# A hybrid attention layer on one core: one ring of six then five load buffers, query and key scalings one step later, distance tables off GpSimd

## The chip, the cores and the metric

The kernel runs on one core of a Trainium2 chip. The metric is the device time of one execution in microseconds (us). The engines are called as the profile calls them: PE is the matmul engine (TensorE), DVE the vector engine (VectorE), ACT the scalar engine (ScalarE), POOL is GpSimd, and SP is the engine (SyncE) whose queue issues the loads.

## The reference

One decoder layer on 256 tokens of width 2048, in float32. A modulation from `c` shifts, scales and gates a normalized input; one projection of 9296 columns feeds two attention groups of eight heads and an indexer of 16 small heads; both groups are gated, joined and projected out.

```python
mod = jax.nn.silu(c) @ w_ada + b_ada
shift, scale, gate = jnp.split(mod, 3, axis=-1)
h = _rms_norm(x, g_norm) * (1.0 + scale[:, None, :]) + shift[:, None, :]
proj = h @ w_in
qa, ka, va, za, q_idx, k_idx, w_idx, qb, kb, vb, zb = jnp.split(proj, COL_SPLITS, axis=-1)
qa = _rms_norm(qa.reshape(heads_a), q_norm_a)      # likewise ka, qb, kb; k_idx over its 64 columns
ya = _dsa_attention(qa, ka, va, q_idx, k_idx, w_idx, _alibi_slopes(N_HEADS_A))
yb = _moba_attention(qb, kb, vb, _alibi_slopes(N_HEADS_B))
ya = ya.reshape(B, L, D_A) * jax.nn.silu(za)
yb = yb.reshape(B, L, D_B) * jax.nn.silu(zb)
y = jnp.concatenate([ya, yb], axis=-1) @ w_out
return x + gate[:, None, :] * y
```

Inside both attentions a score is `q k / sqrt(128) - slope * distance`, masked to the past, with slopes 1/2, 1/4, ... 1/256. The A group sees only the 64 keys that the indexer scores highest for each query. With 256 tokens the B group has one block, so it is plain causal attention.

## The kernel before

**Loads and weights.** All weights come in loads of at most 1 MB, numbered in a fixed order and issued from SP's queue into `raw` buffers (line 244 on, function `issue`). Most loads are pieces of `w_in` or `w_out`, four row tiles of 512 columns each. Others are rows of the transposed `w_ada`; for these one DVE instruction (L289, in the profile CUSTOM_DVE_ANT_0, here called the row product) multiplies a row with silu(c) and adds it up. A weight load is cut into slices of two row tiles, numbered `wh0`, `wl0`, `wh1` and so on: ACT casts a slice to `wh` (L322), DVE subtracts to get the rest `wl` (L332), and PE does three matmuls for each pair of row tile and token tile (L774 to L776), twelve in a slice. ACT and DVE work two slices ahead of PE (`LA = 2`).

**Buffers for loads.** There are four `raw` buffers in one pool and two in a second pool, `rawe`, that only some of the early rows of `w_ada` use. When the indexer starts, `rawe` is closed and its room goes to the small tiles of indexer and heads.

**Work between the slices.** Everything else is written as generators that are stepped between two slices: `idx_k` and eight `idx_pair`s (the indexer; `qi` is a copied query pair, `lg` its matmuls, `rl` their relu), `prep` (norms of queries and keys), `prep_z` and `head`. `yield n` makes a generator skip n further slices. A scheduler then places the written instructions on each engine, so an instruction can stand a little before or behind its place in the text. In `prep` the squares go to ACT (L506), the power -1/2 to GpSimd (L149 and L150), and the eight scalings to ACT (L513):

```python
rsqrt(ssq[:, 8:16], ssq[:, 0:8], HD)
yield 1
...
nc.scalar.activation(s, s, AF.Copy, scale=ssq[:, 8 + 4 * t + h:9 + 4 * t + h])
```

**A head.** `head` transposes queries and keys on PE (`tr`), multiplies them (`s`, L540 and L541), subtracts the slope times the distance on DVE (`ns`, L545) with a table `nb` that GpSimd has made for this head (L536), takes the exponential on ACT (L548), transposes (`pt`, L554), multiplies with the values (`pv`, L563) and makes `yT`, which the output projection needs. Heads are named by group, half and number: `b00` is the first, `a13` the last.

## Time and profile before

| | us |
|---|---|
| Time, median of three runs | 575.06 |
| The three runs | 574.56, 575.06, 578.45 |
| The profiled execution's own time | 578.7 |
| Its span, first to last instruction | 576.9 |
| PE busy | 553.6 |
| DVE busy | 444.5 |
| ACT busy | 319.6 |
| POOL busy | 48.0 |

The span is 1.8 us shorter than the own time of the same execution; nothing in the trace covers that rest. The profiled execution is 3.6 us above the median of the three timed runs and near the longest of them. Busy times of different engines overlap, so they don't add up to the span.

### The profile page before, as it was taken

The numbers are of one execution on the slowest core, as the hardware profiler recorded it, in microseconds if no ns is written. First come the engines' busy times: TensorE is split into PE (matmuls) and PEld (weight loads), VectorE is DVE, ScalarE is ACT, GpSimd is POOL, SyncE is SP. The second block draws the span as 40 slices with busy tenths as digits, with TensorE's granted clock in tenths as the row PEclk, the third lists the DMA queues.
The fourth block names the chain that finished last, engine by engine and source line by source line (L and its number), as shares of the span: only waits on it lengthen the run. The fifth ranks groups of instructions, "written<-read, shape, count | busy, mean of one in ns | idle before, by whom it ended". The sixth has DMA issues, their size and how long they took to land.

```text
span 576.9 us, 7456 instructions
## 1 busy us (share of the span) xinstructions
PE 553.6 (96%) x2658; PEld 462.7 (80%) x2658; DVE 444.5 (77%) x683; ACT 319.6 (55%) x652; POOL 48.0 (8%) x62
## 2 busy tenths in 40 slices
PE   3889999999999999999799999999999999999996
PEld 2769888888889988976577888888888888887885
DVE  4877789898898898998689996678787576458452
ACT  4588563544444353576555566646776785554340
POOL 4100000000000000102201002111110210000000
PEclk9999999999999999999989999999999999999999
DMA  8999998898898987877845376767675468445611
GB/s 293 412 350 370 361 346 326 330 360 285 314 359 318 366 326 270 268 298 279 303 152 177 129 275 235 273 221 265 226 255 201 148 231 279 146 150 190 244 37 38
DMA packets 59670, 150.09 MB, mean 260 GB/s; under 512 B 3056, under 2 KB 9456, under 8 KB 53616
## 3 DMA queue, kind: packets, MB, share of 16 engines
q1 hardware_dynamic: 58480, 147.51, 71.1%
q10 hardware_dynamic: 1152, 2.10, 1.2%
q8 instruction: 21, 0.34, 0.2%
q14 instruction: 17, 0.14, 0.1%
HBM read 147.50 MB, written 2.10 MB: 259 GB/s over the span
## 4 chain that ended last, share of the span: by engine, by line
PE 87%; ACT 4%; DVE 2%; POOL 2%; issue 2%; DMA 1%; SPq 0%; DVEq 0%; ACTq 0%
PE mm_y_o L774 5%; PE mm_y_o L776 5%; PE mm_y_o L775 5%; PE mm_h_zb L776 3%; PE mm_h_zb L774 3%; PE mm_h_zb L775 3%; PE mm_h_za L775 3%; PE mm_h_i L776 3%; PE mm_h_i L775 3%; PE mm_h_i L774 3%; PE mm_h_qb L774 3%; PE mm_h_za L776 3%; PE mm_h_qb L776 3%; PE mm_h_qb L775 3%; PE mm_h_qa L774 3%; PE mm_h_ka L775 2%
## 5 line engine op out<-in xcount | busy, mean ns | idle before, releaser
L322 ACT ACTIVATE wh<-raw 128x1024 fp32r<-128x1024 f32 (+3 forms) x192 | 188.2, 990 | 140.5 <-PE mm_y_o L776 32.9
L332 DVE TENSOR_TENSOR wl<-raw,wh 128x1024 fp32r<-128x1024 f32 (+3 forms) x192 | 215.0, 1140 | 60.5 <-ACT wh L322 59.9
L289 DVE CUSTOM_DVE_ANT_0 raw<-raw,s_row 128x2048 f32<-128x2048 f32 (+1 forms) x49 | 110.2, 2250 | 14.1 <-DMA raw<-in_w_ada_t 14.1
L774 PE MATMUL mm_y_o<-wh,yT 128*128 128x512 f32 x128 | 51.7, 404 | 0.0
L775 PE MATMUL mm_y_o<-wl,yT 128*128 128x512 f32 x128 | 49.9, 390 | 0.0
L776 PE MATMUL mm_y_o<-wh,yT 128*128 128x512 f32 x128 | 49.8, 390 | 0.0
L774 PE MATMUL mm_h_i<-wh,hhi 128*128 128x384 f32 (+1 forms) x96 | 31.7, 330 | 0.0
L775 PE MATMUL mm_h_i<-wl,hhi 128*128 128x384 f32 (+1 forms) x96 | 31.5, 328 | 0.0
L536 POOL TENSOR_SCALAR nbb<-dist 128x384 f32<-128x384 f32 x8 | 8.0, 1001 | 283.3 <-DVE mmod L289 211.2
L776 PE MATMUL mm_h_i<-wh,hlo 128*128 128x384 f32 (+1 forms) x96 | 31.4, 329 | 0.0
L776 PEld LDWEIGHTS mm_y_o<-wh,yT 128*128 128x128 f32 x128 | 24.0, 188 | 5.4 <-DVE yT L575 0.2
L774 PEld LDWEIGHTS mm_y_o<-wh,yT 128*128 128x128 f32 x128 | 24.1, 188 | 4.7 <-ACT yT L574 0.2
L775 PEld LDWEIGHTS mm_y_o<-wl,yT 128*128 128x128 f32 x128 | 24.1, 188 | 4.6
L774 PE MATMUL mm_h_qa<-wh,hhi 128*128 128x512 f32 x64 | 25.6, 409 | 0.9 <-ACT wh L322 0.9
L774 PE MATMUL mm_h_zb<-wh,hhi 128*128 128x512 f32 x64 | 26.4, 412 | 0.0
L774 PE MATMUL mm_h_vb<-wh,hhi 128*128 128x512 f32 x64 | 26.4, 412 | 0.0
L775 PE MATMUL mm_h_za<-wl,hhi 128*128 128x512 f32 x64 | 25.1, 392 | 0.9 <-DVE wl L332 0.9
L774 PE MATMUL mm_h_kb<-wh,hhi 128*128 128x512 f32 x64 | 25.7, 405 | 0.0
L775 PE MATMUL mm_h_zb<-wl,hhi 128*128 128x512 f32 x64 | 25.7, 401 | 0.0
L775 PE MATMUL mm_h_vb<-wl,hhi 128*128 128x512 f32 x64 | 25.6, 400 | 0.0
L774 PE MATMUL mm_h_qb<-wh,hhi 128*128 128x512 f32 x64 | 25.5, 401 | 0.0
L774 PE MATMUL mm_h_za<-wh,hhi 128*128 128x512 f32 x64 | 25.5, 406 | 0.0
(216 smaller groups left out, 1227.3 us busy)
## 6 DMA issues: line engine op xcount, KB each, us to landing
raw<-in_w_in SPq DMA_DIRECT2D x51, 1024.0 KB, 5.9
raw<-in_w_ada_t SPq DMA_DIRECT2D x47, 1024.0 KB, 6.2
raw<-in_w_out SPq DMA_DIRECT2D x16, 1024.0 KB, 5.0
raw<-in_w_in SPq DMA_DIRECT2D x17, 512.0 KB, 3.6
raw<-in_w_in SPq DMA_DIRECT2D x11, 768.0 KB, 4.6
x<-in_x SPq DMA_DIRECT2D x8, 256.0 KB, 6.9
xr<-in_x ACTq DMA_DIRECT2D x8, 256.0 KB, 6.5
raw<-in_w_in SPq DMA_DIRECT2D x3, 672.0 KB, 7.4
```

The costliest lines, as they stand in the source:

```text
L289: nc.vector.tensor_tensor_reduce(out=ld["v"], in0=ld["v"], in1=s_row[:, h0:h1], scale=1.0, scalar=0.0, op0=ALU.mult, op1=ALU.add, accum_ou ...
L322: nc.scalar.activation(hi[:, :n, :w], v, AF.Copy)
L332: nc.vector.tensor_tensor(lo[:, :n, :w], v, sb["hi"][:, :n, :w].bitcast(F32), op=ALU.subtract)
L536: nc.gpsimd.tensor_scalar(nb, dista if q[0] == "a" else dist, 2.0 ** -(hid + 1), 0.0, op0=ALU.mult, op1=ALU.add)
L774: nc.tensor.matmul(ps, a_hi, sb["hi"][:, i, :w], start=st, stop=False)
L775: nc.tensor.matmul(ps, a_hi, sb["lo"][:, i, :w], start=False, stop=False)
L776: nc.tensor.matmul(ps, a_lo, sb["hi"][:, i, :w], start=False, stop=en)
```

## The change

Five things change together.

1. The load buffers are one ring. Up to the indexer load n takes one of six buffers in turn (four of the first pool, two of the second, by `n_issued % 6`). From there on it is one of five: the four, and one that is taken from the room of the small tiles.
2. That room comes from tiles that now share one pair of buffers, tag `qk`: the indexer's `qi`, the tanh tiles `th`, the heads' `qk` and the output's products `o`. The squares of x at the start write to the large pool of `u` tiles instead.
3. `prep` yields 2 instead of 1 before its scalings.
4. The heads' distance tables `nb` are gone. DVE reads the plain distances and multiplies the sum by a constant per head (`scale=`).
5. To make up for that constant, the factor on the keys (`gneg`) is now a table of eight columns, one per head, made by GpSimd at the start: eight memsets and two products, where DVE had two.

```diff
```diff
@@ -45,5 +45,2 @@
 
-EARLY = {1, 2} | set(range(5, 2 * KT + KT * KT))
-
-
 NO_WAIT = mybir.DependencyInfo(mybir.DependencyClass.NoSync, mybir.DependencyReason.DATA)
@@ -139,7 +136,11 @@
         nc.gpsimd.tensor_scalar(one, one, 1.0, None, op0=ALU.add)
+
     gneg = {}
+    steep = consts.tile([P, 8], F32, name="steep")
+    for h in range(8):
+        nc.gpsimd.memset(steep[:, h:h + 1], -(HD ** -0.5) * 2.0 ** (h + 1))
     for i, g in enumerate("ab"):
-        gt = consts.tile([P, 1], F32, name=f"gneg{g}")
-        nc.vector.scalar_tensor_tensor(gt, cc[:, 64 + 2 * i:65 + 2 * i], -(HD ** -0.5),
-                                       cc[:, 65 + 2 * i:66 + 2 * i], op0=ALU.mult, op1=ALU.mult)
+        gt = consts.tile([P, 8], F32, name=f"gneg{g}")
+        nc.gpsimd.tensor_scalar(gt, steep, cc[:, 64 + 2 * i:65 + 2 * i], cc[:, 65 + 2 * i:66 + 2 * i],
+                                op0=ALU.mult, op1=ALU.mult)
         gneg[g] = gt
@@ -246,5 +247,7 @@
             ld = loads[n_issued]
-
-            pool = rawe if ld["kind"] == "ada" and ld["to"][0] == "mod" and n_issued - n_start in EARLY else rawp
-            raw = pool.tile([P, 2048], F32, tag="raw", name=f"raw{n_issued}")
+            pool = rawe if not late_pool and n_issued % 6 > 3 else rawp
+            if late_pool and n_issued % 5 == 4:
+                raw = late_pool[0].tile([P, 2048], F32, tag="raw", bufs=1, name=f"raw{n_issued}")
+            else:
+                raw = pool.tile([P, 2048], F32, tag="raw", name=f"raw{n_issued}")
             if ld["kind"] == "ada":
@@ -352,3 +355,3 @@
         for j in range(4):
-            junk = work.tile([P, 512], F32, name=f"junkx{t}{j}", tag="big", bufs=2)
+            junk = u_tile(f"junkx{t}{j}")
             with in_order():
@@ -466,3 +469,3 @@
             nc.tensor.transpose(pt[:, t * P:(t + 1) * P], proj[g, t][:, c:c + P], ident)
-        qi = late_tiles().tile([P, L], F32, name=f"qi{p}", tag="qi")
+        qi = late_tiles().tile([P, 512], F32, name=f"qi{p}", tag="qk", bufs=2)[:, :L]
         nc.scalar.activation(qi, pt[:, :L], AF.Copy)
@@ -508,3 +511,3 @@
         rsqrt(ssq[:, 8:16], ssq[:, 0:8], HD)
-        yield 1
+        yield 2
         for t in range(2):
@@ -518,3 +521,3 @@
             z = proj["z" + q, t]
-            th = work.tile([P, 512], F32, name=f"th{q}{t}", tag="big", bufs=2)
+            th = late_tiles().tile([P, 512], F32, name=f"th{q}{t}", tag="qk", bufs=2)
             nc.scalar.activation(th, z, AF.Tanh, scale=0.5)
@@ -533,6 +536,5 @@
         nc.vector.tensor_copy(qk[:, :L], pt[:, :L])
-        nc.scalar.activation(qk[:, L:], pt[:, L:], AF.Copy, scale=gneg[q[0]])
-        nb = late_tiles().tile([P, 384], F32, name="nb" + name, tag="nb", bufs=2)
-        nc.gpsimd.tensor_scalar(nb, dista if q[0] == "a" else dist, 2.0 ** -(hid + 1), 0.0,
-                                op0=ALU.mult, op1=ALU.add)
+
+        nc.scalar.activation(qk[:, L:], pt[:, L:], AF.Copy, scale=gneg[q[0]][:, hid:hid + 1])
+        far = dista if q[0] == "a" else dist
         yield 1
@@ -544,3 +546,4 @@
         for t, lo, hi in ((0, 0, P), (1, P, 384)):
-            nc.vector.tensor_tensor_reduce(out=ns[:, lo:hi], in0=ps[:, lo:hi], in1=nb[:, lo:hi], scale=1.0,
+            nc.vector.tensor_tensor_reduce(out=ns[:, lo:hi], in0=ps[:, lo:hi], in1=far[:, lo:hi],
+                                           scale=2.0 ** -(hid + 1),
                                            scalar=3e38, op0=ALU.add, op1=ALU.min, accum_out=st[:, t:t + 1])
@@ -684,3 +687,3 @@
                 for c in range(0, 512, w):
-                    tmp = work.tile([P, 512], F32, name=f"o{n}{t}{c}", tag="big", bufs=2)
+                    tmp = late_tiles().tile([P, 512], F32, name=f"o{n}{t}{c}", tag="qk", bufs=2)
                     nc.vector.tensor_tensor(tmp[:, :w], ps[:, c:c + w], gate_bc[n][:, c:c + w], op=ALU.mult)
```
```

**Where instructions stand now.** Up to about 236 us of the trace the rows of ACT, DVE and SP are the same, apart from the start. Behind that many rows move by one slice. Line numbers below are each kernel's own, three higher in the changed one.

On ACT, around the key norms of the first B half (`jkb` squares, `p_kb` scalings, `qi3` the fourth of the later indexer pairs, for whose matmuls `lg6` PE waits), before:

```order
L506 ACTIVATE jkb013_2532,sskb0_2517<-p_kb0_1_775 128x128
L513 ACTIVATE p_kb0_0_773<-p_kb0_0_773,sskb0_2517 128x128 x3
L468 ACTIVATE qi3_2559<-ptq3_2556 128x256
L513 ACTIVATE p_kb0_0_773<-p_kb0_0_773,sskb0_2517 128x128
L513 ACTIVATE p_kb0_1_775<-p_kb0_1_775,sskb0_2517 128x128 x4
L322 ACTIVATE wh106_2605<-raw98_2398 128x1024
L322 ACTIVATE wh107_2626<-raw98_2398 128x1024
L477 ACTIVATE rl6_2580<-lg6_2577 128x384
L477 ACTIVATE rl7_2587<-lg7_2584 128x384
L322 ACTIVATE wh108_2668<-raw99_2451 128x1024
```

And in the changed kernel:

```order
L509 ACTIVATE jkb013_2541,sskb0_2526<-p_kb0_1_784 128x128
L516 ACTIVATE p_kb0_0_782<-p_kb0_0_782,sskb0_2526 128x128 x2
L325 ACTIVATE wh106_2606<-raw98_2399 128x1024
L471 ACTIVATE qi3_2568<-ptq3_2565 128x256
L516 ACTIVATE p_kb0_0_782<-p_kb0_0_782,sskb0_2526 128x128 x2
L516 ACTIVATE p_kb0_1_784<-p_kb0_1_784,sskb0_2526 128x128 x4
L325 ACTIVATE wh107_2635<-raw98_2399 128x1024
L480 ACTIVATE rl6_2589<-lg6_2586 128x384
L480 ACTIVATE rl7_2596<-lg7_2593 128x384
L325 ACTIVATE wh108_2667<-raw99_2460 128x1024
```

The copy `qi3` still stands behind the first scalings; in front of it there are now two scalings and the cast `wh106`, where there were three scalings.

On PE, the last head, `a13` (some matmuls `mm_y8` of the slices 172 and 174 between these rows are left out), before:

```order
L540 MATMUL sa13_4733<-qka13_4685 128x128
L541 MATMUL sa13_4733<-qka13_4685 128x256
L563 MATMUL pva12_4760<-pTa12_4712,p_va1_0_557 128x256
L565 MATMUL pva12_4760<-pTa12_4712,p_va1_1_559 128x128
L568 MATMUL pva12_4760<-ident_81,p_za1_1_472 128x128
L554 MATMUL pta13_4775<-ident_81,nsa13_4736 128x128 x3
L774 MATMUL mm_y8_o1_0_4566<-wh174_4744,yT4_4588 128x512
L776 MATMUL mm_y8_o1_1_4567<-wh174_4744,yT4_4588 128x512
L774 MATMUL mm_y8_o1_0_4566<-wh174_4744,yT5_4677 128x512
L563 MATMUL pva13_4784<-pTa13_4779,p_va1_0_557 128x256
L568 MATMUL pva13_4784<-ident_81,p_za1_0_470 128x128
```

And in the changed kernel:

```order
L557 MATMUL pta12_4701<-ident_81,nsa12_4642 128x128 x3
L542 MATMUL sa13_4728<-qka13_4682 128x128
L543 MATMUL sa13_4728<-qka13_4682 128x256
L566 MATMUL pva12_4741<-pTa12_4705,p_va1_0_566 128x256
L568 MATMUL pva12_4741<-pTa12_4705,p_va1_1_568 128x128
L557 MATMUL pta13_4752<-ident_81,nsa13_4731 128x128
L778 MATMUL mm_y8_o1_0_4538<-wl174_4714,yT4_4585 128x512
L557 MATMUL pta13_4752<-ident_81,nsa13_4731 128x128 x2
L779 MATMUL mm_y8_o1_0_4538<-wh174_4712,yT4_4585 128x512
L778 MATMUL mm_y8_o1_1_4539<-wl174_4714,yT4_4585 128x512
L566 MATMUL pva13_4761<-pTa13_4756,p_va1_0_566 128x256
L568 MATMUL pva13_4761<-pTa13_4756,p_va1_1_568 128x128
```

All twelve matmuls of slice 172 stood between `sa13` and `pta13`, and now stand ahead of `sa13`; three matmuls of slice 174 stand between the last of `pta13` and `pva13`, where there were seven.

On SP, loads 101 to 108, before:

```order
L276 DMA raw101_2536<-in_w_in 128x4x512
L276 DMA raw102_2599<-in_w_in 128x4x512
L253 DMA raw103_2601<-in_w_ada_t 128x2048
L276 DMA raw104_2666<-in_w_in 128x4x512
L276 DMA raw105_2730<-in_w_in 128x4x512
L253 DMA raw106_2732<-in_w_ada_t 128x2048
L276 DMA raw107_2797<-in_w_in 128x2x512
L276 DMA raw108_2869<-in_w_in 128x4x512
```

And in the changed kernel:

```order
L279 DMA raw101_2545<-in_w_in 128x4x512
L279 DMA raw102_2600<-in_w_in 128x4x512
L256 DMA raw103_2602<-in_w_ada_t 128x2048
L279 DMA raw105_2728<-in_w_in 128x4x512
L256 DMA raw106_2730<-in_w_ada_t 128x2048
L279 DMA raw104_2665<-in_w_in 128x4x512
L279 DMA raw107_2793<-in_w_in 128x2x512
L279 DMA raw108_2853<-in_w_in 128x4x512
```

Load 104, the first to use the buffer from the small tiles' room, is now issued behind 105 and 106.

## Rows read from the trace of the kernel before

**Rows 1.** The page: shares by engine, granted clock in 40 slices, the chain by engine.

```profile
PE 553.6 (96%) x2658; PEld 462.7 (80%) x2658; DVE 444.5 (77%) x683; ACT 319.6 (55%) x652; POOL 48.0 (8%) x62
...
PE 87%; ACT 4%; DVE 2%; POOL 2%; issue 2%; DMA 1%; SPq 0%; DVEq 0%; ACTq 0%
```

**Rows 2.** Waits of the matmul queue, by cause: total us, times, longest us.

```profile
PE lg L474 <- ACT qi L468: 4.4, 2, 3.2
...
PE sb L540 <- ACT rl L477: 0.3, 1, 0.3
PE ptk L457 <- ACT kk L452: 0.2, 1, 0.2
```

**Rows 3.** Busy us of each engine by window, granted clock, DMA share, GB/s.

```profile
0.00:20.00 20.00, 8.37 (x34) 7.59 (x35) 10.91 (x24) 9.86 (x24) 7.99 (x28) 1.00 0.89 326
...
260.00:280.00 20.00, 18.87 (x98) 13.98 (x97) 17.44 (x25) 13.35 (x34) 2.59 (x2) 1.00 0.86 312
280.00:300.00 20.00, 16.61 (x78) 12.37 (x77) 12.49 (x21) 10.32 (x26) 4.18 (x2) 0.91 0.55 180
340.00:560.00 220.00, 219.94 (x1054) 183.14 (x1053) 150.14 (x252) 133.13 (x320) 24.76 (x22) 1.00 0.61 212
560.00:577.00 17.00, 12.51 (x56) 10.02 (x54) 5.20 (x8) 1.07 (x2) 0.00 (x0) 0.93 0.09 32
```

**Rows 4.** Timeline of PE around the longest wait: start us, us, instruction.

```profile
282.91 0.39 PE L776 MATMUL mm_h_vb<-wh,hlo 128*128 128x512 f32 x1
286.54 0.50 PE L474 MATMUL lg<-kiT,qi 64*128 64x128 f32 x4 [3.24 <-ACT qi L468]
```

**Rows 5.** Timeline of ACT, key squares to the fourth copy of the indexer.

```profile
280.46 0.30 ACT L506 ACTIVATE jkb<-p_kb 128x128 f32<-128x128 f32 x1
...
285.24 0.98 ACT L513 ACTIVATE p_kb<-p_kb,sskb 128x128 f32<-128x128 f32 x3 [4.39 <-POOL sskb L150]
286.13 0.36 ACT L468 ACTIVATE qi<-ptq 128x256 f32<-128x256 f32 x1
```

**Rows 6.** Timeline of GpSimd (POOL): powers of eight columns.

```profile
260.17 2.51 POOL L150 TENSOR_TENSOR ssqb<-ssqb,mhalf 128x8 f32<-128x8 f32 x1
...
281.26 3.94 POOL L150 TENSOR_TENSOR sskb<-sskb,mhalf 128x8 f32<-128x8 f32 x1
...
361.62 1.64 POOL L150 TENSOR_TENSOR sskb<-sskb,mhalf 128x8 f32<-128x8 f32 x1
```

**Rows 7.** Timeline of DVE beside the second of these powers.

```profile
281.43 2.28 DVE L289 CUSTOM_DVE_ANT_0 raw<-raw,s_row 128x2048 f32<-128x2048 f32 x1
```

**Rows 8.** Two windows around the longest wait, with the granted clock.

```profile
288.00:292.00 4.00, 4.00 (x14) 3.10 (x12) 3.07 (x5) 2.59 (x4) 0.00 (x0) 0.57 0.02 6
```

**Rows 9.** Timeline of ACT: query scalings, and what follows them.

```profile
262.71 2.45 ACT L513 ACTIVATE p_qb<-p_qb,ssqb 128x128 f32<-128x128 f32 x8 [3.02 <-POOL ssqb L150]
265.07 1.05 ACT L322 ACTIVATE wh<-raw 128x1024 fp32r<-128x1024 f32 x1
...
268.65 0.37 ACT L468 ACTIVATE qi<-ptq 128x256 f32<-128x256 f32 x1
```

**Rows 10.** Groups of GpSimd: the distance tables of the A heads.

```profile
L536 POOL TENSOR_SCALAR nba<-dista 128x384 f32<-128x384 f32 x8 | 8.5, 1066 | 60.6 <-DVE sta L545 44.1 <-DVE stb L545 16.5
```

**Rows 11.** Timeline of GpSimd at the start.

```profile
2.72 1.78 POOL L139 TENSOR_SCALAR cc<-cc 128x1 f32<-128x1 f32 x9 [0.59 <-DMA cc<-in_cols]
...
11.24 0.19 POOL L149 TENSOR_SCALAR rx<-rx 128x1 f32<-128x1 f32 x1 [5.54 <-DVE rx L358]
```

**Rows 12.** Timeline of PE, last head: scores, transposes, products.

```profile
514.79 0.38 PE L540 MATMUL sa<-qka 128*128 128x128 f32 x2
...
521.23 0.67 PE L563 MATMUL pva<-pTa,p_va 128*128 128x256 f32 x2
```

**Rows 13.** Timeline of ACT, last head: second exponential.

```profile
516.49 0.49 ACT L548 ACTIVATE nsa<-nsa,sta 128x256 f32<-128x256 f32 x1
```

**Rows 14.** DMA issues: weight loads, KB each, median us to landing.

```profile
raw<-in_w_in SPq DMA_DIRECT2D x51, 1024.0 KB, 5.9
```

## The prediction

> **What bounds the kernel now.** I read the page's shares first. PE is busy 553.6 of 576.9 us, and 87% of the chain that ended last is PE [rows 1]. So a change pays only where it takes idle time of PE away or gives PE less work, and this one gives PE the same matmuls. The windows say where the idle time lies [rows 3]: 11.63 us in the first 20 us and 4.49 us in the last 17. Neither stretch loses or gains a step on its path, as worked out below. Of the 23.3 us in all this leaves 7.2 us. From 340 to 560 us PE is idle for 0.06 of 220 us, so no weight, load or head is late there. The piece that matters is 260 to 300 us: 1.13 us idle in its first half and 3.39 us in its second.
>
> The waits name the cause [rows 2]: the indexer's matmuls `lg` wait twice for ACT's copy `qi`, 4.4 us together. The longer wait is 3.24 us: `lg6` starts at 286.54 [rows 4]. Followed back: `qi3` is at 286.13 behind three key scalings, and those start at 285.24 after ACT has stood 4.39 us for GpSimd's power; the last squares began at 280.46 [rows 5]. The power was issued at 281.26 and took 3.94 us, while the same power later takes 1.64 us (five times of eight) [rows 6]. Beside it DVE runs a row product from 281.43, for 2.28 us [rows 7]; 1.64 and 2.28 make 3.92, so the power seems to have run behind the row product. After this idle time the clock is granted at 0.57 for four microseconds [rows 8], the lower of its two levels for most of them, which costs 4 x 0.43 = 1.7 us. The stall's whole price is 3.24 + 1.7 = 4.9 us. The window with the shorter wait keeps 1.00 [rows 3].
>
> **Which time the sum starts from.** These rows are of an execution of 578.7 us, 3.6 us above the median and 0.2 us from the longest timed run. The part of the stall that comes from the slow power is 3.94 - 1.64 = 2.3 us, with the clock 4.0 us. That is near 3.6, and the row product started only 0.17 us behind the power. My estimate is that in the two shorter runs the power came first. This is argued, not shown. I make the sum against 578.7 and carry the difference over to 575.06.
>
> **The change part by part.**
>
> Six buffers in one ring, five later. A buffer that is free earlier lets a load start earlier, and that pays only where PE waits for weights. At 0 to 20 us the DMA share is 0.89 [rows 3] and behind that PE waits for nothing that a load brings, save under 2 us; from 340 us on PE has no idle time to give back. I take 0, bounds -0.5 and 0; what covers it is the slices cast two ahead. The cost that it could have is a rival below.
>
> Shared small tiles. `qi`, `th`, `qk` and `o` take turns in two buffers. Each is read within a slice of being written and the next use comes a slice or more later by the order. 0, bounds 0 and 0.4, the length of one `qi` [rows 5].
>
> The factor table. GpSimd gets eight memsets and two products of eight columns. The nearest rows are nine one-column operations in 1.78 us and one of 0.19 us, before which GpSimd stood 5.54 us [rows 11]. Ten times 0.2 is 2 us and fits into the 5.54, so 0; without that cover 2 us would stand in front of the first transposes. DVE loses two tiny operations there: 0.
>
> No distance tables. GpSimd loses 16 operations, 8.5 us for the eight of the A heads [rows 10] and about as much for the others. They were off PE's path, and DVE's operation keeps its shape with another constant. 0 on the path, bounds -0.3 and 0.
>
> Scalings later. Here the order decides, not the number in the yield.
> Query side: `wh100` stood behind the eight query scalings and now stands in front of them, where ACT stood 3.02 us for the power. The cast takes 1.05 us [rows 9]. So `qi1`, at 268.65 after an unbroken row of ACT work, comes up to 1 us earlier, and the wait of 4.4 - 3.24 = 1.16 us falls to some 0.5. But what PE wins here it loses at the next wait unless that one moves too.
> Key side: everything ahead of the squares may run up to 1 us earlier, for the same cast; I take 0.8, since DVE and ACT were without a pause there only in part. Against that `qi3` has the same place behind the power, and in front of it stand two scalings and `wh106` in place of three scalings: 1.05 - 0.98/3 = 0.7 us later. Seen from the start, `lg6` moves by -0.8 + 0.7 = -0.1 us. With the wait for `kk` (0.2 us [rows 2]), whose transposes go one slice later, I take -0.3, bounds -1.3 and +0.7. The power still has the row product behind it, so 3.24 + 1.7 stay in the execution profiled.
>
> A page of the Trainium skill speaks of this pair: "SBUF — State Buffer", section "Who interferes with whom", says that a DVE instruction with two inputs from SBUF and a GpSimd instruction that reads SBUF share a port pair as an exclusive lock, which the first to start holds to its end. By it the power, 0.17 us ahead, should have taken 1.64 us and the row product waited; here the row product took its 2.28 and the power 3.94. By the rule the stall would be 3.24 - 2.3 = 0.9 us, the clock's loss would be gone with it, and this execution would have been near 574.7. The row decides; the issue time of a power may not be the time at which it reads.
>
> Heads one slice later. `sb00` no longer stands in the middle of a crowded slice: its wait of 0.3 us [rows 2] goes, -0.3. At the end it gets tight. Before, scores of `a13` started at 514.79, the second exponential ended at 516.49 + 0.49 = 516.98, and `pva13` came at 521.23 [rows 12, 13]; twelve matmuls filled the time between scores and exponential. Now only `pva12` and one matmul lie there, some 1.1 us against the 2.2 that the chain takes for the last two of the three transposes. I take +0.4 for it, bounds 0 and 2.2.
>
> The sum: -0.3 - 0.3 + 0.4 = -0.2 us. From 578.7 this gives 578.5, and from the median **574.9 us**. The bounds added are -2.4 and +3.0.
>
> **The rivals.**
>
> *The collision goes away (A).* If the new order lets the power run ahead of the row product in all executions, the profiled one gains 4.0 + 0.2 us and comes to 574.5; the median gains only as far as it had the collision, so 570.9 at the best (575.06 - 4.2). For it: 0.17 us is a small distance. Against it: the squares and the row product both hang on the same cast, so they keep their distance. By the Trainium skill's rule on the shared ports ("SBUF — State Buffer", "Who interferes with whom") this is what would happen wherever the power starts first.
>
> *The scalings leave `qi3`'s way (B).* If `qi3` did not wait for the power, all of 4.9 us, 1.16 us and 0.5 us of small waits would go: 575.06 - 6.6 = 568.5. Against it: the order of ACT shows two scalings still in front of `qi3`.
>
> *The collision becomes the rule (C).* Then the median is what the profile is now, 578.5.
>
> *Slower: load 104 is late (D).* It is issued behind 105 and 106, the first of which needs a buffer that a weight slice frees and the second one that a row product frees, and a load takes 5.9 us to land [rows 14]. Between 280 and 300 us DMA is busy 0.55 and DVE 12.49 of 20 us [rows 3], so there is room. It decides once load 104 comes later than the slices ahead of PE last; two loads of 5.9 us are 11.8, of which some 6 would stand on PE, with the clock's 1.7 us: 575.06 + 7.7 = 582.8.
>
> *The change doesn't do what it says (E).* Neither ring nor yield reaches PE and only the tables go; 575.1. In size this can't be told from the forecast.
>
> **How the numbers follow.** Forecast with E 0.64 (572.5 to 577.5), A 0.12, B 0.06, C 0.10, D 0.08. The likeliest time is 574.9. The range leaves out B and D, 0.14, and takes in A and C: 570.5 to 578.6. One per cent is 5.75 us, about what a measurement of this kernel can tell from no change. Faster by more, under 569.3, is B and little else: 0.08. Slower by more, over 580.8, is D with a bad case of C and the tight end: 0.09. Within: 0.83.
>
> **What would show it.** In the changed kernel's profile `lg` should still wait for `qi` for 2 to 4 us near 286 us, with ACT waiting for the power of `sskb`; the shorter wait should be under 1 us, that of `sb` gone, a new one of under 1 us at `pta` or `pva` near 519 us, and PE near 553 us busy. Wrong if no wait for `qi` over 1 us is left (B), if the power takes 1.64 us beside a shorter wait (A), or if PE waits for `wh` or `wl` from slice 114 on (D).

## The result and the profile after

| | us |
|---|---|
| Before, median of 18 runs | 575.33 (573.87 to 578.51) |
| After, median of 18 runs | 579.95 (575.36 to 581.17) |
| After over before | 1.0061, 95% interval 1.0042 to 1.0079 |
| Profiled execution after: own time, span | 579.22, 577.4 |

The change makes the kernel slower: by 0.6% as a ratio, near that of the means (575.92 and 579.29 us), and by 4.6 us by the medians. Forecast were 574.9 us in a range of 570.5 to 578.6; the time lies above the range. Both kernels have two groups of times some 3.5 us apart: of the 18 runs of before twelve lie below 576 and six above 577.7, of after five below 577.6 and thirteen above 579. The medians of the lower groups are 574.8 and 577.0, those of the upper ones 578.3 and 580.2, so either group is some 2 us slower, and the upper one has become the common one. Both profiled executions are of the upper groups and differ by 0.5 us only.

The page of the changed kernel, busy times, chain, and the row products on DVE with their waits:

```profile
PE 554.9 (96%) x2658; PEld 464.1 (80%) x2658; DVE 443.3 (77%) x681; ACT 319.6 (55%) x652; POOL 32.3 (6%) x56
...
PE 90%; ACT 4%; POOL 2%; DMA 1%; issue 1%; DVE 1%; SPq 0%; DVEq 0%
...
L292 DVE CUSTOM_DVE_ANT_0 raw<-raw,s_row 128x2048 f32<-128x2048 f32 (+1 forms) x49 | 109.8, 2240 | 2.8 <-DMA raw<-in_w_ada_t 2.6
```

The row products' line on the page of the kernel before:

```profile
L289 DVE CUSTOM_DVE_ANT_0 raw<-raw,s_row 128x2048 f32<-128x2048 f32 (+1 forms) x49 | 110.2, 2250 | 14.1 <-DMA raw<-in_w_ada_t 14.1
```

PE's share of the chain has grown from 87 to 90% [rows 1], and the row products, which stood 14.1 us for loads before, now stand 2.6 us for them. The ring does what it says, loads come earlier: 1.4 to 3.4 us in the profiles of runs 1, 3, 6 and 10 below, which keep it whole, 6.9 to 14.1 in those without it (before, runs 2, 5 and 7). The waits of PE for ACT's copies, and the windows:

```profile
PE lg L477 <- ACT qi L471: 5.5, 2, 2.8
```

```profile
260.00:280.00 20.00, 17.30 (x84) 12.84 (x85) 15.88 (x23) 11.49 (x29) 4.00 (x1) 0.91 0.65 236
280.00:300.00 20.00, 17.21 (x79) 12.86 (x77) 13.80 (x21) 10.15 (x28) 4.18 (x2) 0.91 0.64 225
340.00:560.00 220.00, 220.00 (x1057) 183.29 (x1056) 150.29 (x252) 132.99 (x324) 11.90 (x12) 1.00 0.60 207
```

The waits for `qi` have grown from 4.4 to 5.5 us [rows 2], and the clock is now lowered in both windows, 0.91 in each, where it was lowered in one [rows 3]; 0.09 of 20 us is 1.8 us. The last head, squeezed as it is, costs nothing: PE is busy for all of 340 to 560 us. PE's two waits, as its timeline has them:

```profile
269.45 0.50 PE L477 MATMUL lg<-kiT,qi 64*128 64x128 f32 x4 [2.70 <-ACT qi L471]
```

```profile
288.00 0.80 PE L477 MATMUL lg<-kiT,qi 64*128 64x128 f32 x4 [2.79 <-ACT qi L471]
```

The second wait is 0.45 us shorter than before [rows 4]; the first is 2.70 us, where it was 4.4 - 3.24 = 1.16 us. Behind it stands a power on GpSimd:

```profile
258.24 5.76 POOL L151 TENSOR_TENSOR ssqb<-ssqb,mhalf 128x8 f32<-128x8 f32 x1
...
282.05 3.95 POOL L151 TENSOR_TENSOR sskb<-sskb,mhalf 128x8 f32<-128x8 f32 x1
```

The power for the queries takes 5.76 us, 3.25 us more than before, and the one for the keys as long as before [rows 6]. Beside the first, DVE:

```profile
254.88 2.28 DVE L292 CUSTOM_DVE_ANT_0 raw<-raw,s_row 128x2048 f32<-128x2048 f32 x1
...
257.08 1.40 DVE L482 SCALAR_TENSOR_TENSOR sc<-rl,w,sc 128x128 f32<-128x128 f32 x4
258.41 0.68 DVE L524 SCALAR_TENSOR_TENSOR p_zb<-thb,p_zb 128x512 f32<-128x512 f32 x1
259.01 3.48 DVE L335 TENSOR_TENSOR wl<-raw,wh 128x1024 fp32r<-128x1024 f32 x3
```

The row product 91 (254.88) stands ahead of the four `sc`; before, it stood behind them and the gating of z:

```profile
255.80 1.42 DVE L479 SCALAR_TENSOR_TENSOR sc<-rl,w,sc 128x128 f32<-128x128 f32 x4 [0.68 <-ACT rl L477]
257.13 0.68 DVE L521 SCALAR_TENSOR_TENSOR p_zb<-thb,p_zb 128x512 f32<-128x512 f32 x1
257.74 2.29 DVE L289 CUSTOM_DVE_ANT_0 raw<-raw,s_row 128x2048 f32<-128x2048 f32 x1
```

So in the changed kernel the squares end and the power is issued (258.24) while the last `sc` runs, and behind it follow the gating and three subtractions without a pause. The run ends at 259.01 + 3.48 = 262.49, the power 1.51 us later, and ACT waits for it:

```profile
264.04 1.28 ACT L516 ACTIVATE p_qb<-p_qb,ssqb 128x128 f32<-128x128 f32 x4 [4.12 <-POOL ssqb L151]
...
269.02 0.37 ACT L471 ACTIVATE qi<-ptq 128x256 f32<-128x256 f32 x1
```

ACT's idle time before the query scalings grew from 3.02 to 4.12 us [rows 9], although the cast `wh100` had been put into it. The scalings start at 264.04 in place of 262.71. `qi1` is only 0.37 us later for that (269.02 in place of 268.65 [rows 9]), since one cast fewer stands between them; the other 1.2 us of the longer wait are PE's, whose last matmul ahead of it started at 266.36 in place of 267.56.

### The profile page after: what moved, and what is told of

Same layout as the page of the kernel before. It is cut to its first block, busy times and chain, and to the rows that moved or that the text cites. A ratio compares the mean times of both kernels' runs of the same rounds, so it can differ in the third digit from the quotient of the medians.

```text
span 577.4 us, 7420 instructions
## 1 busy us (share of the span) xinstructions
PE 554.9 (96%) x2658; PEld 464.1 (80%) x2658; DVE 443.3 (77%) x681; ACT 319.6 (55%) x652; POOL 32.3 (6%) x56
## 4 chain that ended last, share of the span: by engine, by line
PE 90%; ACT 4%; POOL 2%; DMA 1%; issue 1%; DVE 1%; SPq 0%; DVEq 0%
PE mm_y_o L779 5%; PE mm_y_o L777 5%; PE mm_y_o L778 5%; PE mm_h_i L779 3%; PE mm_h_i L778 3%; PE mm_h_i L777 3%; PE mm_h_zb L777 3%; PE mm_h_zb L779 3%; PE mm_h_zb L778 3%; PE mm_h_za L778 3%; PE mm_h_qb L777 3%; PE mm_h_za L779 3%; PE mm_h_qb L779 3%; PE mm_h_qb L778 3%; PE mm_h_qa L777 3%; PE mm_h_ka L778 2%
## 5 line engine op out<-in xcount | busy, mean ns | idle before, releaser
L779 PE MATMUL mm_h_kb<-wh,hlo 128*128 128x512 f32 x64 | 25.7, 402 | 0.0
L778 PE MATMUL mm_h_kb<-wl,hhi 128*128 128x512 f32 x64 | 25.6, 400 | 0.0
L779 PE MATMUL mm_h_zb<-wh,hlo 128*128 128x512 f32 x64 | 25.5, 399 | 0.0
```

What stands on the lines that cost most here:

```text
L778: nc.tensor.matmul(ps, a_hi, sb["lo"][:, i, :w], start=False, stop=False)
L779: nc.tensor.matmul(ps, a_lo, sb["hi"][:, i, :w], start=False, stop=en)
```

## The experiments

Each is compared with runs of the kernel before that were taken beside it on the same chip. Differences between two of the runs below, or to the changed kernel, are of medians, which can come from different chips.

**1. Yield back to 1.** Theory 1 was that the yield, which lets `wh100` and so `wl100` go ahead, made the run on DVE long.

```diff
-        yield 2
+        yield 1
```

> The changed kernel with only the yield in prep put back from 2 to 1; ring, shared tiles and the missing tables stay. Theory 1 (the yield lets the cast wh100 and with it the subtraction wl100 go ahead of the query scalings; the subtraction runs without a pause behind wl98 and wl99 and holds GpSimd's query power back, 5.76 us; the 2.7 us of idle PE that follow lower the clock once more): the query power falls to 2.5 us or less, the first wait for qi to 1.2 us or less with the clock at 1.00 between 260 and 280 us, median 574 to 576. Rival 2 (the ring: row products come earlier and crowd DVE beside the power): no change, power above 5 us, median 579 to 580.5. Rival 3 (heads that are late at the end): no change either, with idle PE behind 340 us.

Measured: 582.73 us, ratio 1.0109 (1.0072 to 1.0145). Theory 1 falls: without the later scalings the kernel is, by the medians, slower still. Rival 2 had the long power, but its time, 579 to 580.5, is too low. The rows of PE's wait and of the query power:

```profile
PE lg L477 <- ACT qi L471: 6.9, 2, 4.7
```

```profile
258.90 6.83 POOL L151 TENSOR_TENSOR ssqb<-ssqb,mhalf 128x8 f32<-128x8 f32 x1
```

Here row product 94 follows `wl99` in place of `wl100`, takes 2.28 us where the subtraction takes 1.2, and the power is longer by that, 6.83 us.

**2. The yield alone.** The kernel before with `yield 2`.

> The kernel before with only the yield in prep set from 1 to 2. Theory 1: the query power above 4.5 us, the first wait for qi above 2 us, median 578 to 580. Rival 2 (the ring): the power and the waits as before, 575.

Measured: 576.18 us, ratio 0.9998 (0.9973 to 1.0023). No change: the yield alone doesn't pay and doesn't cost, as rival 2 had it. The query power:

```profile
259.97 2.51 POOL L150 TENSOR_TENSOR ssqb<-ssqb,mhalf 128x8 f32<-128x8 f32 x1
```

As in the kernel before, though `wl100` is ahead here too. The key power takes 1.75 us: with this yield `wl106` stands between the last `sc` and row product 100.

**3. Copies ahead of the scalings.** An order on ACT only.

```diff
+        last_qi[:] = [nc.scalar.activation(qi, pt[:, :L], AF.Copy)]
...
+                i_s = nc.scalar.activation(s, s, AF.Copy, scale=ssq[:, 8 + 4 * t + h:9 + 4 * t + h])
+                if last_qi:
+                    tc.add_manual_dep(i_s.ins, last_qi[0].ins.name, NO_WAIT, reason="qi first")
```

> The changed kernel with one order added on ACT: the scalings of prep stand behind the indexer copy qi that was written last, so that qi1 and qi3 no longer stand behind the powers. Theory 1 (both waits of PE for qi are ACT standing for the power): both waits go, 2.70 and 2.79 us, and with them both stretches of lower clock, 3.4 us: 579.95 - 8.9 = 571, not above 573.5; the powers may stay long. Rival (ACT and qi are late for another reason, the casts wh101 to wh106 ahead of them): waits of 1 to 2 us stay, 575 to 578.

Measured: 570.54 us, ratio 0.9901 (0.9862 to 0.994). As expected. The windows of this kernel:

```profile
260.00:280.00 20.00, 20.00 (x104) 14.97 (x103) 19.72 (x28) 15.18 (x41) 5.85 (x3) 1.00 0.86 311
280.00:300.00 20.00, 20.00 (x105) 15.03 (x103) 17.64 (x28) 11.21 (x24) 2.85 (x1) 1.00 0.78 272
```

PE has no idle time and no lowered clock left there, and that with a query power of 5.77 us:

```profile
259.03 5.77 POOL L151 TENSOR_TENSOR ssqb<-ssqb,mhalf 128x8 f32<-128x8 f32 x1
```

DVE beside it, from the first of the three subtractions on:

```profile
259.81 3.49 DVE L335 TENSOR_TENSOR wl<-raw,wh 128x1024 fp32r<-128x1024 f32 x3
263.21 1.40 DVE L484 SCALAR_TENSOR_TENSOR sc<-rl,w,sc 128x128 f32<-128x128 f32 x4
```

The power ends at 264.80, again 1.5 us behind the third subtraction, though here DVE goes on without a pause: it is not a pause of DVE that lets it in.

So the long power costs time only by way of ACT's order, `qi` behind scalings that wait for it. This is also the best version of the study.

**4. A probe of the power beside DVE work.** Appended behind the kernel's last instruction: three rounds, each with a power and a run of DVE work let go by the same short memset.

```diff
+        for fn, cnt in ((None, 0), (sub_, 1), (sub_, 2), (sub_, 3), (sub_, 4), (row_, 1), (psum_, 4)):
...
+                nc.vector.memset(sq[:, 0:8], 2.0)
+                nc.gpsimd.tensor_tensor(sq[:, 8:16], sq[:, 0:8], mhalf, op=ALU.pow)
+                for _ in range(cnt):
+                    fn()
+                nc.vector.tensor_copy(acc[:, :8], sq[:, 8:16])
```

> The changed kernel with a probe behind its end: the power of 8 columns on GpSimd, released by a DVE memset, alone and beside 1, 2, 3 and 4 subtractions of 128x1024, one row product, and four additions of 128x512 with one input from PSUM, each three times. The output is not touched. Theory 1 (a run of DVE instructions with two SBUF inputs without a pause keeps GpSimd out until its end): 1.6 us alone, and longer by some 1.1 us with each subtraction, up to 5 to 6 us for four; 3.9 us beside the row product; 1.6 to 2 us beside the four additions. Rival (GpSimd gets in between two DVE instructions): 1.6 to 2.8 us whatever the number of subtractions, 3.9 us beside the row product.

The GpSimd rows of the probe's third round, in the order alone, one and four subtractions, row product, PSUM additions (the rows of two and three subtractions are left out):

```profile
608.19 1.64 POOL L820 TENSOR_TENSOR probe<-probe,mhalf 128x8 f32<-128x8 f32 x1 [1.22 <-DVE probe L819]
610.18 2.48 POOL L820 TENSOR_TENSOR probe<-probe,mhalf 128x8 f32<-128x8 f32 x1 [0.36 <-DVE probe L819]
...
619.59 2.52 POOL L820 TENSOR_TENSOR probe<-probe,mhalf 128x8 f32<-128x8 f32 x1 [1.26 <-DVE probe L819]
624.65 3.65 POOL L820 TENSOR_TENSOR probe<-probe,mhalf 128x8 f32<-128x8 f32 x1 [2.54 <-DVE probe L819]
628.65 1.64 POOL L820 TENSOR_TENSOR probe<-probe,mhalf 128x8 f32<-128x8 f32 x1 [0.36 <-DVE probe L819]
```

2.48 to 2.52 us beside one, two, three or four subtractions, 3.65 beside a row product, 1.64 beside additions with one input from PSUM and 1.64 alone. The rival holds: in isolation the power gets in when the instruction that is running ends. Theory 1 falls a second time.

**5. Old buffers.** The ring taken out, all else as changed.

```diff
-            pool = rawe if not late_pool and n_issued % 6 > 3 else rawp
...
+            pool = rawe if ld["kind"] == "ada" and ld["to"][0] == "mod" and n_issued - n_start in EARLY else rawp
+            raw = pool.tile([P, 2048], F32, tag="raw", name=f"raw{n_issued}")
```

> The changed kernel with only the load buffers put back: four and, for the early rows of w_ada, two more; four later. Yield 2, shared tiles and missing tables stay. Theory 4 (the ring lets row product 91 come early and go ahead of the four sc and the gating of z on DVE; then GpSimd's query power is issued while short DVE instructions run and gets in only behind four further ones): row product 91 stands behind them again, the query power falls from 5.76 to 2.5 us, the first wait for qi to under 0.6 us, median 574.5 to 577. Rival 5 (shared tiles or missing tables): no change, 579 to 580.5.

Measured: 574.75 us, ratio 0.9995 (0.9969 to 1.0021). The first half of theory 4 holds: it is the ring. Row product and powers:

```profile
256.83 2.28 DVE L292 CUSTOM_DVE_ANT_0 raw<-raw,s_row 128x2048 f32<-128x2048 f32 x1
```

```profile
259.25 2.51 POOL L154 TENSOR_TENSOR ssqb<-ssqb,mhalf 128x8 f32<-128x8 f32 x1
...
280.98 1.75 POOL L154 TENSOR_TENSOR sskb<-sskb,mhalf 128x8 f32<-128x8 f32 x1
```

Row product 91 stands behind the gating again, at 256.83, and the two powers take 2.51 and 1.75 us. The key power is short too, which was not expected: in this order `wl106` stands between the last `sc` and row product 100, as in run 2. PE still waits:

```profile
PE lg L477 <- ACT qi L471: 3.3, 1, 3.3
```

The first wait is gone and the second takes 3.3 us; the clock behind it is 0.91 between 280 and 300 us, and 1.00 in the 20 us before.

**6. Only that row product later.** The ring stays; row product 91, and any row product queued behind it, is written only from slice 98 on, and an order puts it behind the gating.

```diff
+        if ld is loads[91]:
+            tc.add_manual_dep(i_row.ins, last_z[0].ins.name, NO_WAIT, reason="row product 91 later")
...
-        while gemv_todo:
...
+        while gemv_todo and not (gemv_todo[0] is loads[91] and j < 98):
```

> The changed kernel with one order added on DVE: row product 91 stands behind the gating of z (as in the kernel before); the subtraction wl98 then goes ahead of the four sc. All else stays, the ring too. Theory 4: the query power no longer stands behind a run of short instructions and three subtractions; it ends 1.3 to 2.5 us earlier, the first wait for qi is 0.2 to 1.4 us instead of 2.7, the clock stays at 1.00 between 260 and 280 us, median 575 to 577.5. Rival (the ring costs by something else than the place of this row product): 579 to 580.5.

Measured: 574.09 us, ratio 0.9979 (0.9954 to 1.0004), 5.9 us below the changed kernel. More than expected, because the key power got short as well:

```profile
260.13 2.51 POOL L151 TENSOR_TENSOR ssqb<-ssqb,mhalf 128x8 f32<-128x8 f32 x1
...
280.19 1.75 POOL L151 TENSOR_TENSOR sskb<-sskb,mhalf 128x8 f32<-128x8 f32 x1
```

```profile
280.65 2.29 DVE L292 CUSTOM_DVE_ANT_0 raw<-raw,s_row 128x2048 f32<-128x2048 f32 x1 [0.22 <-DMA raw<-in_w_ada_t]
```

Row product 100 waited 0.22 us for its load here, and the power got in ahead of it. PE's wait and the windows:

```profile
PE lg L482 <- ACT qi L476: 3.3, 2, 1.7
```

```profile
260.00:280.00 20.00, 18.43 (x97) 13.84 (x94) 17.35 (x26) 13.26 (x38) 2.69 (x3) 1.00 0.78 290
280.00:300.00 20.00, 18.31 (x95) 13.55 (x94) 16.57 (x22) 12.13 (x24) 1.85 (x2) 1.00 0.78 288
```

Against the changed kernel this one removes 2.2 us of waits for `qi` (3.3 in place of 5.5) and both stretches of lower clock, 3.6 us: 5.8. The medians differ by 5.9, the two profiled executions by 5.5. The short key power hangs on the query side: the last of the four `sc` ends at 280.44 in place of 282.31, load 100 lands only some 0.8 us earlier, and so row product 100 is late by 0.22 us where it was in time. So moving this row product takes the whole loss away, more than half of it through that race.

**7. Copies first, in the kernel before** (with `yield 2`).

> The kernel before with yield 2 and with the scalings behind the indexer copy, as in the run with qi first: the waits for qi are gone, the ring, shared tiles and missing tables are not there. If the rest of the change is worth nothing, 570 to 571.5, within 0.2% of that run; if the late heads cost, 1 us less than it; if the ring and the tables help, 1 to 2 us more.

Measured: 571.8 us, ratio 0.9945 (0.9922 to 0.9967). The order on ACT, with the yield, is worth 3 us without ring and changed tables. With them (run 3) the median is 1.3 us lower; the two intervals overlap slightly, so that the rest of the change helps is likely and not shown.

**8 and 11 to 13. Four more probes, for what makes the power wait.** Appended as in 4, with other runs of DVE work, one list for each probe:

```diff
+        for m, cnt in ((0, 0), (0, 1), (0, 2), (0, 4), (1, 4), (2, 1), (2, 2), (2, 4), (4, 4)):
...
+        for fns in ((), (sc_, z_, sub_, sub_, sub_), (sc_, sub_, sub_, sub_), (sc_, row_), (short_, row_),
+                    (short_, z_, sub_, sub_, sub_), (z_, sub_, sub_, sub_), (sc_, z_, sub_, sub_, sub_, sub_, sub_)):
...
+        for at in (0, 1, 2, 3):
+            for fns in ((z_, sub_, sub_, sub_), (sub_, sub_, sub_), (row_,)):
...
+        for what in ("none", "dma", "act", "pe"):
+            for fns in ((sc_, z_, sub_, sub_, sub_), (sc_, row_)):
```

In the first, `m` short additions stand ahead of `cnt` subtractions; in the third, `at` is the place among four `sc` at which both GpSimd operations are let go.

> The second probe behind the end of the changed kernel: the power of 8 columns beside DVE runs that write to different tiles, so that nothing makes them pause: 0, 1, 2 and 4 subtractions of 128x1024, and 1, 2 or 4 short additions of 128x256 ahead of 1, 2 or 4 subtractions, each three times. Theory 4 (a power issued in a short instruction gets in only behind several further ones): 1.6 us alone, 2.5 us beside subtractions alone, and 1 us more with each subtraction up to some 5 to 6 us where short additions stand ahead. Rival (it always gets in at the end of the instruction that is running): 2.5 us or less in all cases.

> The third probe behind the end of the changed kernel: the power of 8 columns is released while a short DVE instruction runs, either the scalar_tensor_tensor of 256 columns that sc is, or a plain addition of 256 columns, or the scalar_tensor_tensor of 512 columns that gates z; behind it come the gating, three or five subtractions to different tiles, or a row product, each three times. If a power that is issued in a scalar_tensor_tensor waits for several further instructions, as by the traces of the kernels: about 5.5 us for sc, gating and three subtractions, 3.9 us for sc and a row product, and 1.7 us where a plain addition stands in the place of sc. Rival (only what stands behind counts): the same in both, 1.7 us before subtractions and 3.9 us before a row product.

> The fourth probe behind the end of the changed kernel: both GpSimd operations of the norm (the tensor_scalar and the power of 8 columns) are released by a memset that stands ahead of the first, second, third or fourth of four sc-like scalar_tensor_tensor of 128 and 256 columns; behind these come the gating of 512 columns and three subtractions, three subtractions alone, or a row product; each three times. It keeps the order of the changed kernel near 258 and 282 us. If the place within the sc decides: the power takes 5 to 6 us ahead of gating and three subtractions and 3.9 us ahead of a row product in at least one of the four places. If the cause is outside DVE and GpSimd's own order (loads, ACT): never above 2.6 us.

> The fifth probe behind the end of the changed kernel: the order that holds the power for 5.76 us in the changed kernel (sc, gating, three subtractions) and the one that holds it for 3.9 us (sc, row product), each twice with nothing else running, with loads running, with casts on ACT running, and with matmuls on PE running. In the earlier probes, with nothing else running, the power took 1.73 us in both. If work beside DVE makes the difference, one of the three backgrounds shows 5 to 6 us and 3.9 us; if none does, 1.7 to 2.6 us in all, and what makes the difference stays open.

In none of these four did a power take more than 3.56 us. With two short additions ahead of subtractions it took 1.68 us; with `sc`, gating and three subtractions 1.73; with `sc` and a row product 1.74; with both GpSimd operations let go among four `sc` 1.74 to 1.96, save the two cases in the rows below; with loads, casts or matmuls beside it 1.69 to 1.81. The third of these probes, GpSimd rows of its second round, where the power is let go at the last `sc` and the run behind it is gating and subtractions, subtractions alone, a row product:

```profile
620.42 1.96 POOL L151 TENSOR_TENSOR probe<-probe,mhalf 128x8 f32<-128x8 f32 x1
...
626.65 2.49 POOL L151 TENSOR_TENSOR probe<-probe,mhalf 128x8 f32<-128x8 f32 x1
...
632.16 3.56 POOL L151 TENSOR_TENSOR probe<-probe,mhalf 128x8 f32<-128x8 f32 x1
```

The fourth, the kernel's own two powers, and two of the probe behind it, with loads running: the first ahead of gating and three subtractions, the second ahead of a row product:

```profile
259.13 5.77 POOL L151 TENSOR_TENSOR ssqb<-ssqb,mhalf 128x8 f32<-128x8 f32 x1
...
282.96 3.95 POOL L151 TENSOR_TENSOR sskb<-sskb,mhalf 128x8 f32<-128x8 f32 x1
...
588.99 1.69 POOL L845 TENSOR_TENSOR probe<-probe,mhalf 128x8 f32<-128x8 f32 x1 [1.60 <-DVE probe L844]
593.85 1.73 POOL L845 TENSOR_TENSOR probe<-probe,mhalf 128x8 f32<-128x8 f32 x1 [3.17 <-DVE probe L844]
```

One execution holds powers of 5.77 and 3.95 us in the kernel and of 1.69 and 1.73 us behind it, with the same kinds of instructions in the same sequence from the last `sc` on. In the probes the power got in at the end of the instruction that ran when it came. The second half of the theory, that a power issued into an `sc` waits for several further instructions by the kind of these, falls.

**9. Six early buffers, four later.**

```diff
-            if late_pool and n_issued % 5 == 4:
-                raw = late_pool[0].tile([P, 2048], F32, tag="raw", bufs=1, name=f"raw{n_issued}")
-            else:
-                raw = pool.tile([P, 2048], F32, tag="raw", name=f"raw{n_issued}")
+            raw = pool.tile([P, 2048], F32, tag="raw", name=f"raw{n_issued}")
```

> The changed kernel without the fifth later buffer: six in one ring up to the indexer, four behind it. Row product 91 stands ahead of the four sc as in the changed kernel. Theory 4 (its place is what costs): as the changed kernel, query power above 5 us, first wait for qi 2.5 to 3 us, median 579 to 581. Rival (the fifth buffer and the late issue of load 104 cost): 575 to 577.

Measured: 576.44 us, ratio 1.0013 (0.9995 to 1.0031). Theory 4 had the power and the first wait (2.7 us), the rival had the time; neither was right alone. The powers:

```profile
258.59 5.77 POOL L151 TENSOR_TENSOR ssqb<-ssqb,mhalf 128x8 f32<-128x8 f32 x1
...
282.35 1.75 POOL L151 TENSOR_TENSOR sskb<-sskb,mhalf 128x8 f32<-128x8 f32 x1
```

The six buffers bring the long query power; the fifth later one brings the long key power, because without it `wl106` stands ahead of row product 100. Without the long key power the kernel is 3.5 us faster than the changed one (579.95 - 576.44), and without the long query power too, as in run 6, another 2.4 (574.09). PE's wait and the first window:

```profile
PE lg L474 <- ACT qi L468: 3.3, 2, 2.7
```

```profile
260.00:280.00 20.00, 17.27 (x84) 12.63 (x83) 15.99 (x22) 11.46 (x30) 4.35 (x1) 0.91 0.74 263
```

The waits add up to 3.3 us here as in runs 5, 6 and 10, all with a key power of 1.75 us, whether the query power takes 2.51 (5 and 6), 4.63 (10) or 5.77 us. By these rows a longer query power moves waiting from the second place to the first and adds none; what it costs is the clock, 0.91 here against 1.00 in the same window of runs 6 and 10.

**10. The last subtraction waits for the power.**

```diff
...
+        if j == 100:
+            tc.add_manual_dep(i_lo.ins, power["b0", "q"].ins.name, SYNC, reason="behind the power")
```

> The changed kernel with one wait added: subtraction wl100 starts only when the query power has ended. Theory 4 (the DVE run up to wl100 is what holds the power): the power gets in behind wl99 or earlier and ends 1.1 us sooner at least, at 4.6 us or less; the first wait for qi falls to 1.6 us or less, median 575.5 to 578. Rival (the power itself is slow there, whatever DVE does): the power stays at 5.8 us, the wait for qi and the median stay or grow, 579.5 to 581.

Measured: 574.67 us, ratio 1.0002 (0.997 to 1.0033), a median lower than expected.

```profile
258.99 4.63 POOL L153 TENSOR_TENSOR ssqb<-ssqb,mhalf 128x8 f32<-128x8 f32 x1
```

The power is 1.13 us shorter, one subtraction's length, and ends 1.5 us behind `wl99`. So the run on DVE does hold it. A wait that is added makes the kernel faster, by 5.3 us by the medians and by 3.3 by the means, since three of its twelve times lie at 578.6 to 581.7. Not all of this is the query power: the key power takes 1.75 us here too, as row product 100 stood for its load as in run 6:

```profile
281.88 2.29 DVE L294 CUSTOM_DVE_ANT_0 raw<-raw,s_row 128x2048 f32<-128x2048 f32 x1 [0.44 <-DMA raw<-in_w_ada_t]
```

## Why the prediction was wrong

**What bounds the kernel** was right. PE's waits for `qi` behind GpSimd's powers, with the lowered clock, are nearly all that was to be won or lost: run 3 removes them and gains 4.4 us on the kernel before and 9.4 on the changed one. The ten profiled kernels (the probes apart) took 571.16 to 582.75 us; with these waits and what the clock cost between 260 and 300 us taken off, 570.1 to 572.5 are left.

**The step that failed** is "Six buffers in one ring, five later ... I take 0, bounds -0.5 and 0." It asked only whether PE waits for weights. An earlier load also releases an earlier row product, and that is a DVE instruction with a place in a queue. Row product 91 went ahead of the indexer's `sc`; the query power then met a run of DVE work and took 5.76 us in place of 2.51, and the clock that fell behind the longer first wait cost 1.8 us, where the step had 0. The fifth later buffer, which puts row product 100 ahead of `wl106`, makes the long key power the common case. Runs 5 and 6 show the first from both sides, run 9 splits the two. The rows of the two kernels' orders that show it, of DVE, were not among those that the prediction rested on; it looked at ACT and PE, and took DVE's row products for moved work off the path.

**The query side** was wrong by sign through the same step. The cast did move into ACT's idle time, as said, but the power ended 1.3 us later, so `qi1` came 0.37 us later where up to 1 us earlier was forecast. PE came 1.2 us earlier, 1.0 us of it from less idle time in the first 20 us, where PE's busy time differs from execution to execution (8.13 to 9.34 us in the five profiles with the whole ring). So the wait went from 1.16 to 2.70 us where 0.5 was forecast, and the clock fell behind it, 1.8 us which the sum did not have.

**The key side**: -0.3 was forecast at `lg6`; its wait fell by 0.45 us, but it starts at 288.00 in place of 286.54 [rows 4], since the loss ahead of it is carried along. That the stall of 4.9 us stays was right for the profile (2.79 + 1.8 us). Of the signs named, the long wait with ACT standing for the power of `sskb` came and the wait for `sb` went; the shorter wait was not under 1 us, and none came at `pta` or `pva`.

**Which time the sum starts from.** For the execution profiled the forecast was 578.5, and that of the changed kernel took 579.22. This nearness is luck: waits and clock came to 2.9 us more (1.1 and 1.8), and less idle time elsewhere, at the start above all, hid most of it. The prediction saw the key power start 0.17 us ahead of the row product and left out the `sc` in which it was issued:

```profile
280.11 1.40 DVE L479 SCALAR_TENSOR_TENSOR sc<-rl,w,sc 128x128 f32<-128x128 f32 x4
```

So the race is not between the power and the row product's start, but whether row product 100 follows the last `sc` at once. In the kernel before, load 100 landed at 280.89, 0.6 us before the last `sc` ended; a load a little later lets the power in, as in runs 6 and 10. The reading that the two groups of times are this collision, present or not, is borne out as far as runs go: the profiles with a long key power ahead of the scalings that PE waits for took 578.7 (before), 579.22 (after) and 582.75 us (run 1), those with a short one (runs 2, 5, 6, 9, 10) 573.69 to 575.98. That it decides each run of before is argued, not shown. Rival C, "the collision becomes the rule", had the shape and was given 0.10; its time of 578.5 lacked the second collision.

**The heads** one slice later: +0.4 was taken; PE has no idle time from 340 to 560 us, so 0. The small waits for `sb` and `kk` went, as said. **Tables, shared tiles, factors**: no cost seen; run 5, which keeps all three, is level with before. **Load 104** (rival D) made no wait.

**What stays open** is why the power does not get in between two instructions of that run, while in five probes of the same instructions it always did. Kind, order, phase, loads, ACT and PE beside it were tried. One difference was not: in the probes a memset on DVE lets the power go and the DVE work waits for no other engine, in the kernels ACT's squares let it go and ACT's casts feed the subtractions. The lengths of the wait in the kernels are sure, the rule is not.

The Trainium skill, "SBUF — State Buffer", section "Who interferes with whom", says that a DVE instruction with two SBUF inputs contends with a GpSimd instruction that reads SBUF, and that one with at most one SBUF input does not, outside DVE's modes that use both port pairs. The probes agree: 2.48 us beside a subtraction, 1.64 beside additions from PSUM. It also says that the first to issue holds the shared ports for its whole instruction. In the changed kernel the power of 258.24 waited for four instructions that started after it, and by this rule it would have waited for the `sc` that ran when it was issued, and for no other. For that place the measurement decides, and the rule is not the whole of it.

## What to carry to other kernels

An earlier transfer isn't free: ask which instruction it releases, on which queue that stands, and what it now goes ahead of. Where a short GpSimd operation stands on the path, see what DVE does while it runs, and take the consumer that PE waits for out from behind it; here one order on ACT is worth more than all five parts of the change. When a kernel's times fall into two groups, look for a race of under a microsecond in the trace before reading a difference of medians.

## What was not expected of the hardware

A power of 128x8 on GpSimd that takes 1.64 us alone took 2.5 us when issued in a subtraction, 3.55 to 3.95 in or just ahead of a row product, and in the kernels 4.63 to 6.83 ahead of gating, subtractions and row product, always ending some 1.5 us behind the instruction that let it in; in the probes it took 1.7 to 2.0 ahead of the same kinds of work.

Idle times of PE of 2.70 and 2.79 us were each followed by a lowered clock (0.91 over 20 us), as was one of 2.16 us in run 1; those of 1.6 and 1.7 us in runs 6 and 10 and one of 2.41 us in run 2 were not (1.00). So the length of one wait does not tell alone whether the clock falls.
